# A six-tick distance between the issue of a load and the issue of its consumer, in a two-layer decoder trunk

## The chip, the cores and the metric

One NeuronCore of a Trainium2 chip runs the whole program. The metric is the device time of one execution in microseconds (us); lower is better. The kernel before took 1227.68 us, the median of three runs that lie between 1226.53 and 1230.73 us.

## What is computed

The reference is a decoder trunk of two layers on 256 tokens of width 1024, in float32. Each layer is a half-step feed-forward block, a token mixer and a second half-step feed-forward block; the mixer is forgetting attention ("fox") in layer 0 and a dilated windowed attention in layer 1. In front of each of these six blocks stands an RMS norm whose result is shifted and scaled, and behind it a gate, and shift, scale and gate come from a conditioning vector c:

```python
for i in range(DEPTH):
    mod = (silu(c) @ mod_w[i] + mod_b[i]).reshape(B, 3, 3, D)
    shift, scale, gate = mod[:, :, 0], mod[:, :, 1], mod[:, :, 2]
    h = modulate(rms_norm(x, norm_g[i, 0]), shift[:, 0], scale[:, 0])
    x = x + 0.5 * gate[:, 0] * swiglu(h, ffn_w_gate[i, 0], ffn_w_up[i, 0], ffn_w_down[i, 0])
    h = modulate(rms_norm(x, norm_g[i, 1]), shift[:, 1], scale[:, 1])
    y = fox_attention(h, ...) if i % 2 == 0 else dilated_attention(h, ...)
    x = x + gate[:, 1] * y
    h = modulate(rms_norm(x, norm_g[i, 2]), shift[:, 2], scale[:, 2])
    x = x + 0.5 * gate[:, 2] * swiglu(h, ffn_w_gate[i, 1], ffn_w_up[i, 1], ffn_w_down[i, 1])
```

All weights and the modulation matrix `mod_w` (2 x 1024 x 9216) are read from HBM once.

## The kernel before

**Products in parts.** Every float32 operand is split into a high part (rounded for the matmul's fast format) and a low part, the rest. A product of two matrices is three matmuls: high by high, high by low and low by high (`mm_blocks`, `mm_wide`, `mm3`, lines 382 to 404). ACT makes the high part of a weight (L207), VectorE (DVE) the low part (L216).

**Weight units.** `Weights` (line 175) holds a plan of all weight tiles in the order of their use, each a unit of up to 128 x 1024 elements. `load` (L189) issues the DMA of the next unit on SP into one of four buffers `raw`; `split_hi` and `split_lo` make `wh` and `wl`, of which there are seven pairs. Loading is tied to splitting: `split_lo` frees a `raw` buffer and calls `load` for the unit four ahead. `need` hands a unit to its products and splits it on the spot if that has not been done.

**Ticks.** The program is written out by Python in the order in which it stands on each engine. `tick` counts a step of the main work (a group of some six to twelve matmuls), lets `advance` issue at most one low and one high split, and then runs the events that `at(delay, ...)` has set for this tick. A tick is no time; it only says where in the program something is issued. PE and SP run strictly in the order of issue. DVE, ACT and GpSimd are arranged by a scheduler, from the same order of issue.

**Modulation steps.** `Mods` (line 257) computes the sixteen vectors of length 1024 that are not made in the opening. A vector takes eight steps. A step (L297) multiplies a 128 x 1024 tile of `mod_w`, in one of two buffers `mraw`, by a column of c and adds it to `acc`; `run` then issues, through `load` (L284), the load after next. When the eighth step is done, `finish` splits `acc` (for a vector of the fox stage: high part on ACT, L319, low part on DVE, L339) and four ticks later `spread` sums it over the partitions with matmuls against ones (L347 and L349, for two halves, four in all). The vectors are consumed by the norm and the gate at the end of a block. A `Pump` (line 363) is called once a unit and issues a step when the count falls behind its share:

```python
def go(self, want):
    if self.done < want and now[0] >= quiet[1]:
        ...
        vectors.run()

def flush(self):
    while self.done < self.n or vectors.open:
        self.go(self.n)
        tick()
```

**The end of a block.** `out_phase` runs the output products of all units but the last four, calls `pump.flush()`, and then runs the last four units' products half by half, with the gate, the sum and the next norm between them (`Boundary`). What `flush` issues on PE, the spread matmuls of the last vector among it, stands ahead of those last products.

**Fox.** The stage lasts from about 222 to 350 us. Its 24 modulation steps, the vectors (0,1,2), (0,2,0) and (0,2,1), are shared over 32 units. The attention of each group of four heads is issued by events: logits (L1140, L1141), the masked sum with its maximum on DVE (L960), the exponent on ACT (L962), transposes (L972), the values (L986), the reciprocal of the sums on DVE (L990), its spread by transposes (L1000), and the normalized output (L1003) with its low part (L1007).

Of the kernel before, what the change touches and what calls it, by code (L numbers as in the profile page):

```python
# [47 lines left out]
WBUFS = 7  # L48
# [12 lines left out]
NORM_FOX = 5  # L61
NORM_DIL = 10
RAWS = 4
AHEAD = 5
RI_DELAY = 1
QUIET0 = 5
# [26 lines left out]
def trunk_kernel(ctx, tc, x_in, c_in, positions, mod_w, mod_b, norm_g, w_gate, w_up, w_down,  # L93
# [25 lines left out]
    now = [0]  # L119
# [17 lines left out]
    def spread_out(delay, steps):  # L137

        def run():
            try:  # L140
                next(steps)
                at(2, run)
            except StopIteration:
                pass
        at(delay, run)

    def dram(t, off, ap):
        return bass.AP(tensor=t.tensor, offset=t.offset + off, ap=ap)
# [24 lines left out]
    quiet = [0, 0]  # L173

    class Weights:


        def __init__(self):
            self.plan, self.raws, self.parts, self.stamps = [], [], [], []
            self.loaded = self.hi = self.lo = self.used = self.live = 0  # L180
            self.started = False
            self.extra, self.spare = set(), None

        def load(self):
            if self.loaded < len(self.plan):
                shape, loads = self.plan[self.loaded]
                raw = rawp.tile([P] + shape, F32, tag="raw", bufs=RAWS, name="raw")
                for view, src in loads(raw):
                    nc.sync.dma_start(view, src)  # L189
                self.raws.append(raw)  # L190
                self.loaded += 1

        def start(self):
            self.started = True
            for _ in range(RAWS):
                self.load()
# [23 lines left out]
        def advance(self):  # L220
            if self.started and now[0] >= quiet[0]:
                if self.lo < self.hi and self.stamps[self.lo] < now[0]:
                    self.split_lo()
                spare = sum(i in self.extra for i in range(self.used, self.hi + 1))
                if self.hi < min(self.used + AHEAD + spare, self.loaded) and (
                        self.live < WBUFS or self.hi in self.extra):
                    self.split_hi()

        def need(self):
# [7 lines left out]
        def release(self):  # L237
            def run():
                self.live -= 1
            at(0, run)  # L240
# [4 lines left out]
    def behind(key, on=True):  # L245
        return tc.issue_after(ahead[key]) if on and key in ahead else ExitStack()
# [10 lines left out]
    class Mods:  # L257


        def __init__(self, order):  # L260
            self.steps = [(v, k) for v in order for k in range(KT)]
            self.loaded, self.done, self.open = 0, 0, 0
            self.raws = deque()

        def start(self):
            z = main.tile([P, D], F32, name="bias")
# [12 lines left out]
        def load(self):  # L279
            if self.loaded < len(self.steps):  # L280
                (l, s, j), k = self.steps[self.loaded]
                col = (s * 3 + j) * D
                raw = rawp.tile([P, D], F32, tag="mraw", bufs=2, name="mraw")
                nc.sync.dma_start(raw, mod_w[l, k * P:(k + 1) * P, col:col + D])  # L284
                self.raws.append(raw)
                self.loaded += 1

        def run(self):
            v, k = self.steps[self.done]
            l, s, j = v  # L290
            if k == 0:
                assert not self.open
                self.open += 1
                self.acc = main.tile([P, D], F32, tag="acc", bufs=1, name="acc")
            acc, raw = self.acc, self.raws.popleft()
            with behind("dve"):
                dve.scalar_tensor_tensor(acc, raw, ccol[:, k:k + 1], self.bias_tile if k == 0 else acc,  # L297
                                         op0=OP.mult, op1=OP.add)
            self.done += 1
            self.load()  # L300
            if k == 0:
                self.bias(self.done - 1 + KT)
            elif k == 2:
                dst = main.tile([P, D], F32, tag=f"mod{j}", name=f"mod{j}")
                if j == 1:
                    nc.sync.dma_start(dst, dram(norm_g, (l * 3 + s) * D, [[0, P], [1, D]]))
                mods[v] = dst
            elif k == KT - 1:
                self.finish(v, acc)
# [52 lines left out]
    class Pump:  # L362
# [7 lines left out]
            self.go(min(self.n, -(-self.n * self.seen // self.units)))  # L370

        def go(self, want):
            if self.done < want and now[0] >= quiet[1]:
                if vectors.open and vectors.steps[vectors.done][1] == 0:
                    return
                vectors.run()
                self.done += 1
# [6 lines left out]
    vectors = Mods(MODS_A + MODS_FOX + MODS_B + MODS_B2 + MODS_DIL + MODS_C)  # L384
# [322 lines left out]
    def open_trunk(wg, wu, pool):  # L707
# [54 lines left out]
        def load_weights(q):  # L762
            k0, n = groups[q]
            for k in range(k0, k0 + n):
                rows = slice(k * P, (k + 1) * P)
                raw = rawp.tile([P, 2, 512], F32, tag="raw", bufs=RAWS, name="raw")
                nc.sync.dma_start(raw[:, 0], wg[rows, 0:512])
                nc.sync.dma_start(raw[:, 1], wu[rows, 0:512])
                ws[0, k] = raw
                if k % 2 == 0:  # L770
                    raw = rawp.tile([P, 2, 512], F32, tag="raw", bufs=RAWS, name="raw")
                    nc.sync.dma_start(raw, wg[k * P:(k + 2) * P, 512:1024].rearrange("(k p) n -> p k n", p=P))
# [682 lines left out]
```

## Time and profile before

| what | value |
|---|---|
| median of three runs | 1227.68 us |
| the profiled execution | 1226.56 us |
| its span, first to last instruction | 1224.8 us |
| PE (TensorE matmul) busy | 1202.1 us, 98% |
| DVE (VectorE) busy | 952.3 us, 78% |
| ACT (ScalarE) busy | 665.0 us, 54% |
| read from HBM | 277.71 MB, 228 GB/s over the span |
| modulation loads: count, size, issue to landing | 128, 512 KB, 5.0 us |

PE counts matmuls as busy from their start to their modelled end, and neighbours overlap, so small gaps don't show in the share. The time of a wait is put down to the engine, or the DMA, whose signal came last. The profile's own execution is 1.1 us under the median.

### The profile page before, as it was taken

The numbers are of one execution on the slowest core, as the hardware profiler recorded it, in microseconds if no ns is written. First come the engines' busy times: TensorE is split into PE (matmuls) and PEld (weight loads), VectorE is DVE, ScalarE is ACT, GpSimd is POOL, SyncE is SP. The second block draws the span as 40 slices with busy tenths as digits, with TensorE's granted clock in tenths as the row PEclk, the third lists the DMA queues.
The fourth block names the chain that finished last, engine by engine and source line by source line (L and its number), as shares of the span: only waits on it lengthen the run. The fifth ranks groups of instructions, "written<-read, shape, count | busy, mean of one in ns | idle before, by whom it ended". The sixth has DMA issues, their size and how long they took to land.

```text
span 1224.8 us, 20467 instructions
## 1 busy us (share of the span) xinstructions
PE 1202.1 (98%) x7810; PEld 1071.1 (87%) x7810; DVE 952.3 (78%) x1362; ACT 665.0 (54%) x1038; POOL 99.0 (8%) x130
## 2 busy tenths in 40 slices
PE   6999999999999999999999999999999999999998
PEld 5999988878779999889999887888888787888887
DVE  7878777998788788569987659978786778877753
ACT  4446444576654555444554436577575655655540
POOL 1000000223100000001000004121131100000000
PEclk9999999999999999999999999999999999999999
DMA  9879986695839988638889656655645652877561
GB/s 332 274 260 341 307 306 196 190 309 192 283 98 345 324 275 311 212 111 288 307 270 331 205 172 215 214 190 165 225 146 188 207 172 86 273 215 221 172 214 41
DMA packets 162306, 281.16 MB, mean 230 GB/s; under 512 B 13424, under 2 KB 99984, under 8 KB 162208
## 3 DMA queue, kind: packets, MB, share of 16 engines
q1 hardware_dynamic: 162208, 279.85, 69.1%
q8 instruction: 61, 1.00, 0.3%
q14 instruction: 37, 0.30, 0.1%
HBM read 277.71 MB, written 2.10 MB: 228 GB/s over the span
## 4 chain that ended last, share of the span: by engine, by line
PE 78%; DVE 7%; DMA 5%; issue 4%; ACT 3%; POOL 2%; SPq 1%; POOLq 0%; DVEq 0%; ACTq 0%
PE bank L402 12%; PE bank L403 12%; PE bank L404 12%; PE block_bank L390 10%; PE block_bank L392 10%; PE block_bank L391 10%; PE block_bank L398 6%; PE block_bank L399 3%; DMA mraw<-in_mod_w_dram 3%; DVE wl L216 2%; POOL hrs L896 1%; ACT wh L207 1%; DVE lo L960 1%; DVE acc L297 1%; PE obank L986 1%
## 5 line engine op out<-in xcount | busy, mean ns | idle before, releaser
L216 DVE TENSOR_TENSOR wl<-raw,wh 128x1024 fp32r<-128x1024 f32 (+1 forms) x360 | 434.5, 1215 | 142.0 <-ACT wh L207 138.2
L207 ACT CAST wh<-raw 128x1024 fp32r<-128x1024 f32 (+1 forms) x360 | 374.0, 1045 | 263.2 <-PE bank L404 103.3
L390 PE MATMUL block_bank<-hT,wh 128*128 128x256 f32 x992 | 281.8, 284 | 2.0 <-ACT hT L819 2.0
L392 PE MATMUL block_bank<-hT,wl 128*128 128x256 f32 x992 | 281.7, 284 | 0.0
L391 PE MATMUL block_bank<-hT,wh 128*128 128x256 f32 x992 | 280.8, 283 | 0.0
L402 PE MATMUL bank<-wh,hT 128*128 128x512 f32 (+2 forms) x496 | 191.4, 386 | 1.1 <-DVE nm L960 0.7
L390 PEld LDWEIGHTS block_bank<-hT,wh 128*128 128x128 f32 x992 | 188.4, 190 | 2.4 <-ACT hT L819 2.1
L391 PEld LDWEIGHTS block_bank<-hT,wh 128*128 128x128 f32 x992 | 188.2, 190 | 0.5 <-DVE hT L822 0.2
L392 PEld LDWEIGHTS block_bank<-hT,wl 128*128 128x128 f32 x992 | 187.8, 189 | 0.0
L404 PE MATMUL bank<-wh,hT 128*128 128x512 f32 (+2 forms) x496 | 181.6, 366 | 0.0
L403 PE MATMUL bank<-wl,hT 128*128 128x512 f32 (+2 forms) x496 | 181.0, 365 | 0.0
L297 DVE SCALAR_TENSOR_TENSOR acc<-mraw,ccols,acc 128x1024 f32<-128x1024 f32 x112 | 143.3, 1280 | 31.5 <-DMA mraw<-in_mod_w_dram 31.3
L403 PE MATMUL bank<-wl,aTh 128*128 128x512 f32 (+1 forms) x420 | 146.4, 349 | 0.0
L402 PE MATMUL bank<-wh,aTh 128*128 128x512 f32 (+1 forms) x420 | 146.1, 348 | 0.0
L404 PE MATMUL bank<-wh,aTl 128*128 128x512 f32 (+1 forms) x420 | 145.7, 347 | 0.0
L398 PE MATMUL block_bank<-hT,wh 128*128 128x512 f32 x320 | 112.6, 394 | 0.0
L404 PEld LDWEIGHTS bank<-wh,hT 128*128 128x128 f32 x496 | 93.3, 188 | 16.5 <-DVE hT L479 0.5
L402 PEld LDWEIGHTS bank<-wh,hT 128*128 128x128 f32 x496 | 93.6, 189 | 15.8 <-issue 2.1
L403 PEld LDWEIGHTS bank<-wl,hT 128*128 128x128 f32 x496 | 93.7, 189 | 12.7
L399 PE MATMUL block_bank<-hT,wl 128*128 128x256 f32 x320 | 90.5, 283 | 0.0
L402 PEld LDWEIGHTS bank<-wh,aTh 128*128 128x128 f32 x420 | 79.5, 189 | 10.9
L404 PEld LDWEIGHTS bank<-wh,aTl 128*128 128x128 f32 x420 | 79.3, 189 | 10.5
(236 smaller groups left out, 1551.7 us busy)
## 6 DMA issues: line engine op xcount, KB each, us to landing
mraw<-in_mod_w_dram SPq DMA_DIRECT2D x128, 512.0 KB, 5.0
raw<-in_ffn_w_down_dram SPq DMA_DIRECT2D x88, 512.0 KB, 4.1
raw<-in_ffn_w_gate_dram SPq DMA_DIRECT2D x76, 512.0 KB, 4.6
raw<-in_ffn_w_up_dram SPq DMA_DIRECT2D x76, 512.0 KB, 4.2
raw<-in_dil_w_in_dram SPq DMA_DIRECT2D x128, 256.0 KB, 3.9
raw<-in_fox_w_in_dram SPq DMA_DIRECT2D x36, 256.0 KB, 4.3
oraw<-in_mod_w_dram SPq DMA_DIRECT2D x32, 256.0 KB, 6.3
raw<-in_ffn_w_gate_dram SPq DMA_DIRECT2D x24, 256.0 KB, 6.1
```

The costliest lines, as they stand in the source:

```text
L207: act.copy(wh, self.raws[self.hi])
L216: dve.tensor_sub(wl, self.raws[self.lo], wh.bitcast(F32))
L297: dve.scalar_tensor_tensor(acc, raw, ccol[:, k:k + 1], self.bias_tile if k == 0 else acc, op0=OP.mult, op1=OP.add)
L390: pe.matmul(out_i, wh[:, blk], hTh[:, :, k, :], start=first and i % 2 == 0, stop=False)
L391: pe.matmul(out_i, wh[:, blk], hTl[:, :, k, :], start=False, stop=False)
L392: pe.matmul(out_i, wl[:, blk], hTh[:, :, k, :], start=False, stop=last and i % 2 == 1)
L398: pe.matmul(o[i], wh[:, blk], hT[:, :, :, k, :], start=first, stop=False)
L399: pe.matmul(o[i][:, 0], wl[:, blk], hTh[:, :, k, :], start=False, stop=last)
L402: pe.matmul(o, ah, wh, start=first, stop=False)
L403: pe.matmul(o, ah, wl, start=False, stop=False)
L404: pe.matmul(o, al, wh, start=False, stop=last)
L896: nc.gpsimd.tensor_tensor(rs, ms, mhalf, op=OP.pow)
```

## The change

A constant `LANDED = 6` is added, and `Weights` and `Mods` note the tick at which each load is issued. `advance` issues the high split of a unit only if its load was issued six ticks ago or more; `need` still splits at once. The pump runs a modulation step only if the oldest load that no step has used was issued six ticks ago or more. `flush` keeps calling the pump, one tick at a time, until all steps of the stage are done. Nothing else is changed: the loads, the buffers, the splits and the steps are the same instructions, and only their places move.

```diff
--- before.py
+++ after.py
@@ -61,6 +61,7 @@
 NORM_FOX = 5
 NORM_DIL = 10
 RAWS = 4
+LANDED = 6
 AHEAD = 5
 RI_DELAY = 1
 QUIET0 = 5
@@ -176,7 +177,7 @@
 
 
         def __init__(self):
-            self.plan, self.raws, self.parts, self.stamps = [], [], [], []
+            self.plan, self.raws, self.parts, self.stamps, self.issued = [], [], [], [], []
             self.loaded = self.hi = self.lo = self.used = self.live = 0
             self.started = False
             self.extra, self.spare = set(), None
@@ -188,6 +189,7 @@
                 for view, src in loads(raw):
                     nc.sync.dma_start(view, src)
                 self.raws.append(raw)
+                self.issued.append(now[0])
                 self.loaded += 1
 
         def start(self):
@@ -223,7 +225,8 @@
                     self.split_lo()
                 spare = sum(i in self.extra for i in range(self.used, self.hi + 1))
                 if self.hi < min(self.used + AHEAD + spare, self.loaded) and (
-                        self.live < WBUFS or self.hi in self.extra):
+                        self.live < WBUFS or self.hi in self.extra) and (
+                        now[0] - self.issued[self.hi] >= LANDED):
                     self.split_hi()
 
         def need(self):
@@ -260,7 +263,10 @@
         def __init__(self, order):
             self.steps = [(v, k) for v in order for k in range(KT)]
             self.loaded, self.done, self.open = 0, 0, 0
-            self.raws = deque()
+            self.raws, self.issued = deque(), deque()
+
+        def landed(self):
+            return now[0] - self.issued[0] >= LANDED
 
         def start(self):
             z = main.tile([P, D], F32, name="bias")
@@ -283,6 +289,7 @@
                 raw = rawp.tile([P, D], F32, tag="mraw", bufs=2, name="mraw")
                 nc.sync.dma_start(raw, mod_w[l, k * P:(k + 1) * P, col:col + D])
                 self.raws.append(raw)
+                self.issued.append(now[0])
                 self.loaded += 1
 
         def run(self):
@@ -293,6 +300,7 @@
                 self.open += 1
                 self.acc = main.tile([P, D], F32, tag="acc", bufs=1, name="acc")
             acc, raw = self.acc, self.raws.popleft()
+            self.issued.popleft()
             with behind("dve"):
                 dve.scalar_tensor_tensor(acc, raw, ccol[:, k:k + 1], self.bias_tile if k == 0 else acc,
                                          op0=OP.mult, op1=OP.add)
@@ -370,7 +378,7 @@
             self.go(min(self.n, -(-self.n * self.seen // self.units)))
 
         def go(self, want):
-            if self.done < want and now[0] >= quiet[1]:
+            if self.done < want and now[0] >= quiet[1] and vectors.landed():
                 if vectors.open and vectors.steps[vectors.done][1] == 0:
                     return
                 vectors.run()
```

Line numbers of the change are higher than those before by 1 from line 64 on, by 2 from line 191, by 3 from line 227, by 6 from line 264, by 7 from line 286 and by 8 from line 296 on: L297 is L305 there, L339 is L347, L347 and L349 are L355 and L357, L1003 is L1011.

First piece: DVE at the end of the fox stage, from the last masked sum of the attention (`lo`) to the spread vector (`mod`). `acc` is the accumulator of a modulation step, `mraw` its loaded tile, `ri` the reciprocal, `on` and `oTl` the normalized heads. Before:

```order
L297 SCALAR_TENSOR_TENSOR acc<-mraw,ccols,acc 128x1024
L960 ISA lo,nm<-bank,table_972 128x256
L960 ISA nm 128x1
L339 TENSOR_TENSOR wl<-acc,wh 128x1024
L990 RECIPROCAL ri<-sums 128x8
L216 TENSOR_TENSOR wl<-raw,wh 128x1024
L351 SCALAR_TENSOR_TENSOR mod_3709<-bank,mod_3709 128x512
L1003 TENSOR_TENSOR on<-obank,on 128x512
```

With the change:

```order
L968 ISA lo,nm<-bank,table_953 128x256
L968 ISA nm 128x1
L218 TENSOR_TENSOR wl<-raw,wh 128x1024
L998 RECIPROCAL ri<-sums 128x8
L305 SCALAR_TENSOR_TENSOR acc<-mraw,ccols,acc 128x1024
L1011 TENSOR_TENSOR on<-obank,on 128x512
L305 SCALAR_TENSOR_TENSOR acc<-mraw,ccols,acc 128x1024
L1015 TENSOR_TENSOR oTl_2474<-on,oTh_2472 128x256
L1015 TENSOR_TENSOR oTl_2475<-on,oTh_2473 128x256
L305 SCALAR_TENSOR_TENSOR acc<-mraw,ccols,acc 128x1024 x4
L347 TENSOR_TENSOR wl<-acc,wh 128x1024
L218 TENSOR_TENSOR wl<-raw,wh 128x1024
```

Before, the last step and its low part (L339) stand ahead of the reciprocal; with the change six steps stand behind it, and the low part behind them.

Second piece: PE at the same place, from the transposes of the last head to the first product of the last four output units. Before:

```order
L972 MATMUL bank_3903<-ident,lo 128x128 x2
L986 MATMUL obank<-pt,v_3698 64x128 x4
L986 MATMUL obank<-pt,v_3699 64x128 x2
L1000 MATMUL rbank<-ident,wide 128x128 x4
L347 MATMUL bank<-wh,ones 128x512
L349 MATMUL bank<-wl,ones 128x512
L347 MATMUL bank<-wh,ones 128x512
L349 MATMUL bank<-wl,ones 128x512
L402 MATMUL bank<-wh,oTh_2472 128x512
```

With the change:

```order
L980 MATMUL bank_3870<-ident,lo 128x128 x2
L355 MATMUL bank<-wh,ones 128x512
L357 MATMUL bank<-wl,ones 128x512
L355 MATMUL bank<-wh,ones 128x512
L357 MATMUL bank<-wl,ones 128x512
L994 MATMUL obank<-pt,v_3672 64x128 x4
L994 MATMUL obank<-pt,v_3673 64x128 x2
L1008 MATMUL rbank<-ident,wide 128x128 x4
L355 MATMUL bank<-wh,ones 128x512
L357 MATMUL bank<-wl,ones 128x512
L355 MATMUL bank<-wh,ones 128x512
L357 MATMUL bank<-wl,ones 128x512
```

The spread of the vector (0,2,0) has moved down to here; the spread of the last vector, (0,2,1), and the products behind it keep their places. The only other move on PE is the spread of (0,1,2), some 70 matmuls later in the same stage.

Third piece: SP at the same place, where it issues the loads of modulation tiles among those of the next block's weights. Before:

```order
L284 DMA mraw<-in_mod_w_dram 128x1024
L189 DMA raw<-in_ffn_w_gate_dram 128x2x512
L284 DMA mraw<-in_mod_w_dram 128x1024 x2
L189 DMA raw<-in_ffn_w_gate_dram 128x2x512 x2
L189 DMA raw<-in_ffn_w_up_dram 128x2x512 x4
```

With the change:

```order
L290 DMA mraw<-in_mod_w_dram 128x1024
L283 DMA bias<-in_mod_b_dram 1x1024
L190 DMA raw<-in_ffn_w_gate_dram 128x2x512
L290 DMA mraw<-in_mod_w_dram 128x1024 x2
L314 DMA mod_3919<-in_norm_g_dram 128x1024
L290 DMA mraw<-in_mod_w_dram 128x1024 x5
L190 DMA raw<-in_ffn_w_gate_dram 128x2x512 x2
```

Seven loads of modulation tiles now stand between two loads of weights, where two stood.

## Rows read from the trace of the kernel before

**Rows 1.** The page, parts 1 and 4: busy time, and the chain that ended last.
```profile
PE 1202.1 (98%) x7810; PEld 1071.1 (87%) x7810; DVE 952.3 (78%) x1362; ACT 665.0 (54%) x1038; POOL 99.0 (8%) x130
...
PE 78%; DVE 7%; DMA 5%; issue 4%; ACT 3%; POOL 2%; SPq 1%; POOLq 0%; DVEq 0%; ACTq 0%
```
**Rows 2.** Windows, first feed-forward block and fox: stretch, length, each engine's busy us.
```profile
core 0: us, PE busy (x) PEld busy (x) DVE busy (x) ACT busy (x) POOL busy (x), PEclk, DMA share, GB/s
...
60.00:222.00 162.00, 161.98 (x1153) 152.23 (x1152) 128.89 (x135) 81.38 (x101) 3.55 (x7) 1.00 0.78 269
222.00:290.00 68.00, 65.83 (x386) 54.83 (x386) 61.95 (x102) 46.06 (x96) 16.50 (x12) 1.00 0.87 282
290.00:350.00 60.00, 57.89 (x379) 47.00 (x380) 45.89 (x88) 37.85 (x99) 10.34 (x17) 1.00 0.59 198
```
**Rows 3.** Waits of PE, 222 to 350 us: us in total, times, longest.
```profile
PE bank L921 <- DVE qn L900: 1.2, 1, 1.2
PE obank L986 <- ACT pt L974: 0.8, 1, 0.8
PE bank L402 <- DVE nm L960: 0.7, 1, 0.7
PE bank L1140 <- DVE ncum L1133: 0.6, 1, 0.6
PE bank L972 <- DVE nm L960: 0.5, 1, 0.5
PE bank L349 <- DVE wl L339: 0.3, 1, 0.3
PE bank L1140 <- DVE nm L960: 0.2, 1, 0.2
```
**Rows 4.** Waits of DVE for modulation loads: the whole run, then 222 to 350 us.
```profile
DVE acc L297 <- DMA mraw<-in_mod_w_dram: 31.3, 21, 3.5
...
DVE acc L297 <- DMA mraw<-in_mod_w_dram: 6.5, 3, 3.4
```
**Rows 5.** Timeline of DVE at the end of fox: start us, us, instruction [idle before].
```profile
308.50 1.28 DVE L297 SCALAR_TENSOR_TENSOR acc<-mraw,ccols,acc 128x1024 f32<-128x1024 f32 x1 [3.37 <-DMA mraw<-in_mod_w_dram]
...
328.60 1.28 DVE L297 SCALAR_TENSOR_TENSOR acc<-mraw,ccols,acc 128x1024 f32<-128x1024 f32 x1 [1.08 <-DMA mraw<-in_mod_w_dram]
...
335.62 1.23 DVE L339 TENSOR_TENSOR wl<-acc,wh 128x1024 fp32r<-128x1024 f32 x1 [0.77 <-ACT wh L319]
336.76 0.20 DVE L990 RECIPROCAL ri<-sums 128x8 f32<-128x8 f32 x1
...
341.23 0.68 DVE L1003 TENSOR_TENSOR on<-obank,on 128x512 f32<-128x512 f32 x1
...
342.43 0.75 DVE L1007 TENSOR_TENSOR oTl<-on,oTh 128x256 fp32r<-128x256 f32 x2
```
**Rows 6.** The chain that ended last, 318 to 346 us: start us, us, what.
```profile
339.53 0.59 PE rbank L1000 x4
340.12 0.23 PE bank L347
...
340.82 0.24 PE bank L349
341.06 0.23 PE bank L402
```
**Rows 7.** All uses of the tile mraw: durations min/median/max, and its loads.
```profile
L297 DVE SCALAR_TENSOR_TENSOR acc<-mraw,ccols,acc x112: 1267/1279/1308, 73.2 to 1122.7; 128x1024 f32<-128x1024 f32 x112
...
DMA to landing us min/median/max: 3.7/5.0/7.9
```
**Rows 8.** Timeline of ACT at the end of fox.
```profile
334.54 1.05 ACT L319 CAST wh<-acc 128x1024 fp32r<-128x1024 f32 x1 [0.95 <-DVE acc L297]
```
**Rows 9.** Windows in the opening, columns as in group 2.
```profile
19.90:24.80 4.90, 4.84 (x21) 4.64 (x22) 4.41 (x8) 1.31 (x3) 0.00 (x0) 1.00 1.07 373
24.90:29.80 4.90, 4.90 (x44) 4.90 (x44) 4.83 (x11) 1.64 (x2) 0.00 (x0) 1.00 1.09 355
```

## Prediction

> **What bounds the kernel now.** I read the busy shares first: TensorE is busy for 98% of the span, and the chain that ended last is 78% PE, 7% DVE and 5% DMA [rows 1]. So time can be won only where PE waits, and lost wherever something new makes it wait. The table by stage says where that is: from 60 to 222 us, the first feed-forward block, PE is busy for 161.98 of 162.00 us; in the forgetting attention (fox) it misses 2.17 us of 68 and 2.11 of 60 [rows 2]. The waits of PE in the fox stage show seven waits, 4.3 us together, none behind a DMA directly [rows 3]. VectorE does wait for the modulation loads: 31.3 us over the run, but only 6.5 of that in fox, where PE can feel it [rows 4]. Two of those waits reach PE: the steps that start at 308.50 and 328.60 stood 3.37 and 1.08 us idle before them [rows 5], and the logits behind them on DVE hold PE for 0.7 and 0.5 us [rows 3].
>
> **The change part by part.** It removes no instruction and adds none; a load keeps its size and each step its operation. It moves the point at which a step enters the program, and that is read from the built order.
>
> *Splits.* In the feed-forward and dilated stages they move by a tick or so, and the PE order there is unchanged. At the first block the splits of units 0 to 4 are issued 5 to 8 ticks later, yet on DVE the splits of the first six units stay ahead of all modulation steps. What hides them is that PE runs these blocks without a gap [rows 2] and splits stay at least one tick ahead of their use. I cost them at nothing; if that cover were gone, each late unit would cost at most one split of 1.2 us. In the dilated stage the modulation steps keep their ticks: they come six ticks or more apart already. No gain there.
>
> *Modulation steps in fox.* The pump spreads 24 steps over 32 units of two ticks, one each 2.7 ticks. There are two load buffers, and a step's run issues the load after next; with the gate a pair of steps takes six ticks or more, three per step, and the pump never catches up. When the output phase flushes the pump, 22 of 24 steps were issued before; with the change 16 are. All eight steps of the last vector (call them 40 to 47) then stand together. On PE nothing has given way: the four matmuls that spread this vector still stand behind the transposes of the last heads and ahead of the 48 products of the last four output units, as the second piece of order shows. PE takes them in order.
>
> So the chain is: load, step, load, step, through two buffers. I follow it on the clock of the trace. Steps 40 and 41 fall between the last logits and start the loads of 42 and 43, which land before they are wanted. Step 42 stands behind the reciprocal, which ends at 336.96 [rows 5]; a step takes 1.28 us [rows 7], so it ends at 338.3 and releases load 44. Step 43 stands behind the product of L1003, which ends at 341.91 [rows 5]: it ends at 343.2 and releases load 45. The two low parts (L1007) take 0.75 us [rows 5], and step 44 follows to 345.2, releasing load 46. From there each load counts from issue to landing: 3.7 us at least, 5.0 median, 7.9 at most [rows 7]. I take 4.4, between the least and the median, because SP has nothing to issue in this stretch except these loads. Load 45 lands at 347.6, step 45 ends at 348.9; load 46 lands at 349.6, step 46 ends at 350.9; load 47, released at 348.9, lands at 353.3 and step 47 ends at 354.6. Then come ACT's cast, 1.05 us [rows 8], the low part on DVE, 1.23 us [rows 5], and after the first spread matmul three more of 0.23 us [rows 6]. The last products start at 357.6 instead of 341.06 [rows 6]: **+16.5 us**. With 3.7 us landings (two on the path) it is +15.1, with 5.0 it is +17.7, with 7.9 it is +23.5.
>
> *The clock.* In that wait PE has nothing between the end of the last transposes at 340.12 [rows 6] and 355.65, some 15.5 us. The trace before has no such idle stretch once PE runs. Its nearest row is the start: after a beginning with little work PE issues 21 matmuls in the 4.9 us from 19.9, and 44 in the 4.9 us from 24.9 [rows 9], about half the pace, as the 1.2 GHz level gives against 2.4; the clock column reads 1.00 in both rows, so I go by the pace. That is worth 4.9 x (1 - 21/44) = 2.6 us. The ends are 0, if the clock stays, and 2.6; I take 2.6, since 15.5 us idle is nearer to the idle start than to a stage without gaps. By the Trainium skill, "TensorE: Matmul & The Clock Gate", section "What's actually happening", the slow level is what an idle PE returns to and work releases it; by it the 2.6 stay in the sum, but no row here shows the clock falling a second time inside the run.
>
> *What is won.* The two PE waits behind late modulation loads in fox, 0.7 + 0.5 = **-1.2 us** [rows 3]; at most all 4.3.
>
> The sum is 16.5 + 2.6 - 1.2 = **+17.9 us**. The profiled execution took 1226.56 us (its span is 1224.8), so it would become 1244.5. The median of the runs before, 1227.68, lies 1.1 above it; on the median I forecast **1245.5 us**.
>
> **The rivals.** *Hidden, and faster.* DVE no longer stands in front of unlanded data, and its 31.3 us of waiting [rows 4] goes. The Trainium skill, "DMA: Bandwidth & Descriptors", section "Rules for kernel authors", tells authors to issue a DMA early, compute, and wait for it late, and the gate does wait later. By that rule alone the time would fall; but here the run of a step is also what issues a later load, so the gate delays issues as well as waits. In rows: PE could get back 1.2 to 4.3 us in fox [rows 3], for 1223.4 to 1226.5, say 1223.5. It decides in the flush: step 47 would have to end before PE ends the last transposes at 340.12 [rows 6]. Against it, two steps and two whole landings still follow step 43, which cannot end before 343.2. Chance 0.03.
>
> *No difference.* The late steps and the saved waits cancel, within 0.3% (about 3.7 us, what a measurement of this kernel can tell from no change). It would need a stall of under 5 us in the flush, where one landing with its step is 5 already and there are two. Chance 0.04.
>
> *The clock stays.* All as forecast, without the 2.6: 1242.9 us. For it speaks that the clock is shown only at full level after the start, against it that PE was never idle so long. Chance 0.15.
>
> *Contended loads.* The loads in the flush take the 7.9 us of the longest row [rows 7], because weight loads for the next block are still being moved: +7.0, so 1252.5 us. Against it, the four weight buffers fill early and their next loads wait for splits. Chance 0.08.
>
> The forecast itself keeps 0.70.
>
> **How the numbers follow.** The low end takes landings of 3.7 (-1.4), no fall of the clock (-2.6) and all 4.3 us of PE waits won (-3.1): +10.8, or 1238.5; rounded down, 1238. The high end takes landings of 5.0 (+1.2), nothing won (+1.2) and one longest landing on the path in place of a median one (+2.9): +23.2, or 1251. The forecast and the case with the clock at full level lie inside, 0.85 together. Slower by over 0.3%: 0.70 + 0.15 + 0.08 = 0.93. Within 0.3%: 0.04. Faster: 0.03.
>
> **What the profile of the change would show.** On PE, one idle stretch of about 15 us at the end of fox, in front of the spread matmuls, released by the cast of the accumulator or by its low part, and the same order as before around it. On DVE, four steps in a row there with two waits of 2 to 4 us for the modulation load, and hardly any wait for it earlier in fox. After the stretch, products at half pace for some us if the clock falls. From 60 to 222 us and in the dilated stage, PE as busy as before. I am wrong if that stretch is under 5 us, if PE waits for split weights in a feed-forward block, or if the time is gained back in the dilated stage.

## Result, and the profile after

The change takes 1242.72 us, the median of four runs (1241.27 to 1243.61), against 1227.99 us for the kernel before in the same session: a ratio of 1.0116, 95% interval 1.0096 to 1.0137. It is slower by 14.7 us; forecast were 1245.5 us, in a range of 1238 to 1251, and slower. The profiled execution of the change took 1243.61 us, its span is 1241.9.

The page of the change, parts 1, 2 (one row) and 4, answers to [rows 1]:

```profile
PE 1203.3 (97%) x7810; PEld 1070.7 (86%) x7810; DVE 952.5 (77%) x1362; ACT 665.3 (54%) x1038; POOL 96.1 (8%) x130
...
PEclk8999999999979999999999999999999999999999
...
PE 76%; DVE 8%; DMA 6%; issue 4%; ACT 3%; POOL 2%; SPq 1%; POOLq 0%; DVEq 0%; ACTq 0%
```

The work is the same to the instruction, and PE is busy 1.2 us longer in a span 17.1 us longer: it waits. One slice in forty has a granted clock of 7 tenths; before, no slice inside the run fell. The windows place both (columns as in [rows 2]):

```profile
core 0: us, PE busy (x) PEld busy (x) DVE busy (x) ACT busy (x) POOL busy (x), PEclk, DMA share, GB/s
60.00:222.00 162.00, 161.99 (x1152) 152.15 (x1151) 128.41 (x134) 81.44 (x100) 3.56 (x7) 1.00 0.79 268
...
341.00:352.00 11.00, 0.57 (x1) 0.29 (x1) 5.71 (x6) 1.66 (x2) 0.00 (x0) 0.50 0.72 198
352.00:358.00 6.00, 5.53 (x14) 4.15 (x14) 4.25 (x5) 1.37 (x2) 0.00 (x0) 0.50 0.61 174
358.00:365.00 7.00, 7.00 (x32) 5.71 (x31) 4.62 (x8) 1.45 (x4) 0.55 (x1) 1.00 0.18 67
```

The first feed-forward block is as full as before. From 341 to 352 us PE runs a single matmul, and the granted clock is at its lower level, 1.2 GHz; in the next six us it runs 14 matmuls at 1.2 GHz, and only then is the clock back at 2.4. The waits of PE from 222 to 366 us answer to [rows 3] (us in total, times, longest):

```profile
PE bank L355 <- ACT wh L327: 13.6, 1, 13.6
PE bank L980 <- ACT lo L970: 1.0, 2, 0.7
```

The two waits of 0.7 and 0.5 us behind the attention's maximum [rows 3] are gone, 1.0 us behind its exponent is new, and one of 13.6 us is there: the spread of the last vector waits for the high part of the accumulator. DVE's waits for modulation loads, in the whole run and then from 222 to 366 us:

```profile
DVE acc L305 <- DMA mraw<-in_mod_w_dram: 34.8, 25, 3.1
...
DVE acc L305 <- DMA mraw<-in_mod_w_dram: 8.0, 6, 1.8
```

The gate was to keep steps away from loads that have not landed, yet the total is 34.8 us where it was 31.3 [rows 4]; a second profile of the change (experiment 6) has 33.3. The timeline of DVE at the end of fox shows where the waits are now (start, us, instruction, idle before it):

```profile
339.13 1.27 DVE L305 SCALAR_TENSOR_TENSOR acc<-mraw,ccols,acc 128x1024 f32<-128x1024 f32 x1
340.32 0.75 DVE L1015 TENSOR_TENSOR oTl<-on,oTh 128x256 fp32r<-128x256 f32 x2
340.99 1.28 DVE L305 SCALAR_TENSOR_TENSOR acc<-mraw,ccols,acc 128x1024 f32<-128x1024 f32 x1
344.04 1.28 DVE L305 SCALAR_TENSOR_TENSOR acc<-mraw,ccols,acc 128x1024 f32<-128x1024 f32 x1 [1.77 <-DMA mraw<-in_mod_w_dram]
346.63 1.28 DVE L305 SCALAR_TENSOR_TENSOR acc<-mraw,ccols,acc 128x1024 f32<-128x1024 f32 x1 [1.31 <-DMA mraw<-in_mod_w_dram]
349.02 1.28 DVE L305 SCALAR_TENSOR_TENSOR acc<-mraw,ccols,acc 128x1024 f32<-128x1024 f32 x1 [1.10 <-DMA mraw<-in_mod_w_dram]
351.41 1.23 DVE L347 TENSOR_TENSOR wl<-acc,wh 128x1024 fp32r<-128x1024 f32 x1 [1.11 <-ACT wh L327]
```

Steps 43 to 47 stand here, all but the first behind the low parts of the last heads (L1015), the last three each behind a load. The chain that ended last goes through every second of them (start, us, what):

```profile
337.22 0.60 PE rbank L1008 x4
...
340.43 3.51 DMA mraw<-in_mod_w_dram
...
344.04 1.30 DVE acc L305
...
345.35 3.58 DMA mraw<-in_mod_w_dram
...
349.02 1.29 DVE acc L305
...
350.34 1.05 ACT wh L327
...
351.41 1.24 DVE wl L347
...
352.69 0.79 PE bank L357
353.49 0.43 PE bank L355
353.92 0.43 PE bank L357
354.34 0.43 PE bank L410
```

Step 43 ends and load 45 is issued; it lands, step 45 runs, load 47 is issued; it lands, step 47 runs; then cast, low part, spread, and the first product at 354.34, where it stood at 341.06 [rows 6].

Where the time lies can be read from the start of the same matmul in both profiles. One at the end of the first feed-forward block is 0.4 us earlier (222.25 and 221.88 us), one at the end of fox's output 14.8 later (350.37 and 365.14), one at the end of the third feed-forward block still 14.7 later (731.38 and 746.09), the last of all 17.0 later (1220.85 and 1237.89). Fox costs 15.1 us, the feed-forward blocks nothing; 2.3 us more come in the dilated stage of this execution.

### The profile page after: what moved, and what is told of

The parts are those of the page before. It is cut to its first block, busy times and chain, and to the rows that moved or that the text cites. A ratio compares the mean times of both kernels' runs of the same rounds, so it can differ in the third digit from the quotient of the medians.

```text
span 1241.9 us, 20469 instructions
## 1 busy us (share of the span) xinstructions
PE 1203.3 (97%) x7810; PEld 1070.7 (86%) x7810; DVE 952.5 (77%) x1362; ACT 665.3 (54%) x1038; POOL 96.1 (8%) x130
## 4 chain that ended last, share of the span: by engine, by line
PE 76%; DVE 8%; DMA 6%; issue 4%; ACT 3%; POOL 2%; SPq 1%; POOLq 0%; DVEq 0%; ACTq 0%
PE bank L410 11%; PE bank L411 11%; PE bank L412 11%; PE block_bank L400 9%; PE block_bank L398 9%; PE block_bank L399 9%; PE block_bank L406 6%; DMA mraw<-in_mod_w_dram 3%; PE block_bank L407 3%; DVE wl L218 3%; POOL hrs L904 1%; DMA raw<-in_dil_w_in_dram 1%; PE obank L994 1%; PE bank L980 1%; DVE acc L305 1%
## 5 line engine op out<-in xcount | busy, mean ns | idle before, releaser
L305 DVE SCALAR_TENSOR_TENSOR acc<-mraw,ccols,acc 128x1024 f32<-128x1024 f32 x112 | 143.4, 1281 | 35.1 <-DMA mraw<-in_mod_w_dram 34.8
```

## Experiments

The theory is the one of the prediction: with two buffers, and a step that issues the load after next, the gate limits the pump to two steps in six ticks, eight steps are left for the flush, and there they run at the pace of load and step ahead of PE's last products. The rivals: the gate on splits is to blame; the empty ticks of the longer flush are; the idle PE's clock is most of it; the loads themselves are slow there. Each ratio is against runs of the kernel before on the same chip in the same session.

**1. Only the splits gated.**

```diff
-            if self.done < want and now[0] >= quiet[1] and vectors.landed():
+            if self.done < want and now[0] >= quiet[1]:
```

> Only the splits of weight units keep the gate; modulation steps run as before. The backlog theory (the lost time is the eight modulation steps left for the flush of the fox stage) expects the time of before, within 0.3% (1224 to 1232 us), 22 of 24 steps issued at the flush, and no PE wait over 2 us at the end of fox. The rival that late splits cost time expects a part of the 14.7 us here, 3 us or more, with PE waiting behind the low part of a split. For the 2.3 us by which the dilated stage became longer: if they come from the splits' places, they are here too.

Measured: 1229.18 us, ratio 1.0014 (1.0004 to 1.0024), +1.7 us by the ratio; 22 of 24 steps are issued when fox is flushed, and the longest PE wait in fox is 1.4 us. The splits are not the cause of the loss; by the median they are not quite free either.

**2. Only the steps gated.**

```diff
-                        self.live < WBUFS or self.hi in self.extra) and (
-                        now[0] - self.issued[self.hi] >= LANDED):
+                        self.live < WBUFS or self.hi in self.extra):
```

> Only the modulation steps keep the gate; splits are issued as before. The backlog theory expects the time of the change, 1240 to 1245 us, with the one PE wait of 12 to 15 us ahead of the last spread matmuls of fox and the clock down behind it. The rival of late splits expects 3 us or more less than the change. If the 2.3 us in the dilated stage are here and not in the run with gated splits alone, they come with the steps.

Measured: 1241.63 us, 1.0124 (1.0108 to 1.0139), and the wait of PE is there to the tenth:

```profile
PE bank L354 <- ACT wh L326: 13.6, 1, 13.6
```

The steps carry the whole loss.

**3. Steps gated, but the flush calls them without the gate**, so it takes 13 ticks and not 25.

```diff
-        def go(self, want):
-            if self.done < want and now[0] >= quiet[1] and vectors.landed():
+        def go(self, want, late=False):
+            if self.done < want and now[0] >= quiet[1] and (late or vectors.landed()):
...
-                self.go(self.n)
+                self.go(self.n, True)
```

> The change, but the flush issues its steps without asking for the six ticks: it takes 13 ticks in place of 25. The eight steps are still left for it. The backlog theory (real loads through two buffers set the wait, ticks set none) expects the time of the change, 1240 to 1245 us, and a PE wait of 12 to 15 us. The rival that the flush's own ticks cost the time expects half of it back, about 1235 us.

Measured: 1242.8 us, 1.0129 (1.0114 to 1.0144), one PE wait of 13.9 us. Empty ticks cost nothing; the steps that are left over do.

**4. The distance: four ticks for both, four and eight for the steps alone.**

```diff
-LANDED = 6
+LANDED = 4
```

> The change with a distance of four ticks in place of six, for splits and steps: a pair of steps in four ticks, two a step, which is faster than the 2.7 that the pump asks for, so 22 of 24 steps are issued at the flush, as before. The backlog theory expects the time of before or up to 0.3% less (1222 to 1231 us) and no PE wait over 2 us at the end of fox. The rival that any gate costs, by moving steps on DVE, expects 5 us or more of the loss to stay.

Measured: 1226.62 us, 0.9998 (0.9988 to 1.0007), 22 of 24 steps issued at the flush, no PE wait in fox over 1.4 us.

> Only the steps gated, at four ticks: 22 of 24 issued at the flush, splits as before. The backlog theory expects no difference from before that is over 0.3%. If data that has landed when its step comes up is worth something, it shows here and nowhere else: DVE's 31.3 us of waits for modulation loads should fall, and PE's two waits behind them, 1.2 us, should go: 1225 to 1227 us. If waits of DVE that PE does not feel are worth nothing, the time is that of before.

Measured: 1227.73 us, 1.0005 (0.9996 to 1.0014). The gain that a gate should bring without a backlog does not come. Nor did it remove waits; DVE's over the run, which were 31.3 in 21 [rows 4], with the steps alone gated (36.2 with both gates at four ticks):

```profile
DVE acc L304 <- DMA mraw<-in_mod_w_dram: 33.3, 23, 3.8
```

With `LANDED = 8` and the steps alone:

> Only the steps gated, at eight ticks in place of six: 14 of 24 steps are issued at the flush of fox, ten are left, and at the flush of the first feed-forward block two are left where none was. The backlog theory prices a further pair of steps through two buffers at 4.9 us (3.5 landing, 1.28 step and the hand-overs, as in the profile of the change), and the two steps in the first block at 1 to 5 us of cast, low part and spread: 1246 to 1254 us. A rival by which the wait in fox is a fixed price of the flush expects 1242 us.

Measured: 1248.57 us, 1.0169 (1.0151 to 1.0187). 14 of 24 steps are issued at fox's flush, and the first feed-forward block has a backlog of its own, 22 of 24; the end of that block comes 4.6 us later than before. Both show as waits of PE:

```profile
PE bank L354 <- ACT wh L326: 15.7, 1, 15.7
...
PE bank L354 <- DVE wh L340: 3.1, 1, 3.1
```

With the steps alone gated, four, six and eight ticks leave two, eight and ten steps to the flush of fox. In one profile each, the stage is 2.5, 15.5 (experiment 2) and 18.5 us longer than before. The 2.5 are not at the flush but ahead of it (see the last section), and the median of that version is the one of before; stages of single profiles differ by some 2 us (experiment 6). The fifth pair cost 3.0 us, not the 4.9 expected, and the chain of the eight-tick run shows that no third landing was added (start, us, what):

```profile
345.23 1.27 DVE acc L304
...
347.18 1.21 DVE acc L304
...
348.40 4.76 DMA mraw<-in_mod_w_dram
...
353.25 1.29 DVE acc L304
...
354.56 3.50 DMA mraw<-in_mod_w_dram
...
358.16 1.29 DVE acc L304
```

Two landings are on the path, as in the change. What is longer is the stretch ahead of the first, where steps 42 and 43 now both stand behind the product of the last heads (`on`), by 1.9 us, and the landings themselves, 4.85 and 3.60 to the start of the step, by 1.2.

**5. The clock: PE filled with unread matmuls while the steps run.** Their results are used by nothing. First 54, three in a tick:

```diff
         def flush(self):
+            start, db = now[0], None
...
+                if now[0] > start + 7:
+                    db = db or bank()
+                    for _ in range(3):
+                        pe.matmul(db, ones, hTh[:, 0, 0:4, :].rearrange("p k n -> p (k n)"), start=True, stop=True)
```

> The change, with 54 matmuls of 512 columns that nobody reads, issued on PE in the flush of fox between the last transposes and the last spread: 54 x 0.232 = 12.5 us of the 13.6 us that PE waits there. If the granted clock fell because PE was idle, it stays up, the 12 or so matmuls behind the wait run at 0.232 in place of 0.43 us, and the time falls by 2 to 3 us, to about 1240 us. If the clock falls for another reason, the time is that of the change, 1242 to 1243 us. Added work, nothing left out.

Measured: 1245.59 us, 1.0146 (1.0131 to 1.0162). Inconclusive: the fill was too short. It ended at 349.97 us, the high part was ready only at 352.93, the clock fell in between, and three of the unread matmuls stood behind the spread, where they cost time. The second version puts 64 ahead of the spread:

```diff
+                if start + 8 < now[0] and vectors.open:
+                    db = db or bank()
+                    for _ in range(4):
+                        pe.matmul(db, ones, hTh[:, 0, 0:4, :].rearrange("p k n -> p (k n)"), start=True, stop=True)
```

> As the run with 54 unread matmuls, but 64 of them, all ahead of the last spread: 64 x 0.232 = 14.8 us, which covers the wait of 13 to 15 us to its end. If idleness of PE lowers the clock, there is now no stretch at half pace behind the wait, the first products run at 0.232 us, and the time is 2 to 3 us below that of the change (about 1240 us). If the clock falls all the same, or the fill delays the spread by more than it saves, it is 1242 us or more. Added work, nothing left out.

Measured: 1240.06 us, 1.0107 (1.0093 to 1.0121). Windows, and the timeline of PE:

```profile
341.00:352.00 11.00, 11.00 (x49) 9.03 (x49) 5.98 (x7) 0.29 (x1) 0.00 (x0) 1.00 0.69 203
352.00:358.00 6.00, 5.24 (x22) 3.86 (x21) 4.89 (x6) 3.05 (x3) 0.00 (x0) 1.00 0.52 145
```

```profile
338.89 14.92 PE L395 MATMUL bank<-hT,ones 128*128 128x512 f32 x64
...
355.71 0.40 PE L415 MATMUL bank<-wh,oTh 128*128 128x512 f32 x1
355.95 0.39 PE L416 MATMUL bank<-wl,oTh 128*128 128x512 f32 x1
```

The clock stays at 2.4 GHz, and products follow each other after 0.23 us, not 0.43. The first of them even starts 1.5 us later than in the change, yet fox is 0.9 us shorter than in the first profile of the change, and 2.6 shorter than in the second. The median is 2.7 us lower; by the ratios, each to its own session, it is 1.1 us against the first measurement of the change and 2.8 against its repeat (experiment 6), with overlapping intervals. So the size rests on the trace; that it is a small part of the loss, and that the wait for the steps is the large one, both measurements say.

**6. The change again**, without an edit.

> The change itself once more, for a second profile. In the first, the dilated stage was 2.3 us longer than before, though its modulation steps keep their ticks. If that is the changed order of DVE and ACT there, it comes back within 0.5 us; if it is a difference between executions, the second profile shows another number. The wait at the end of fox should be 13 to 14.5 us again.

Measured: 1243.17 us, 1.0130 (1.0112 to 1.0149), a PE wait of 14.6 us; fox costs 16.8 us in this profile and the dilated stage 0.6; with the steps alone gated (experiment 2) that stage is 1.2 us shorter than before. So the 2.3 us of the first profile in the dilated stage differ between executions and are no effect of the change that these runs can tell.

**7. A third load buffer in the fox stage.** With both gates left at six ticks, every third load of the stage goes to a buffer of its own:

```diff
+                if self.third and self.loaded % 3 == 2:
+                    if self.loaded >= 48:
+                        return
+                    raw = self.third.tile([P, D], F32, tag="mraw3", bufs=1, name="mraw3")
+                else:
+                    raw = rawp.tile([P, D], F32, tag="mraw", bufs=2, name="mraw")
...
         pump = Pump(MODS_FOX, PUMP_FOX)
+        vectors.third = pool
+        vectors.load()
```

> The change with six ticks kept everywhere, and a third buffer for modulation tiles in the fox stage alone: three steps in six ticks, two a step, so 22 of 24 are issued at the flush. The backlog theory (rate = buffers over distance) expects the time of before within 0.3% (1224 to 1231 us) and no PE wait over 2 us at the end of fox, though every step still waits its six ticks. The rival that the six ticks themselves cost the time expects 1240 us or more.

Measured: 1230.8 us, 1.0031 (1.0021 to 1.0041). 22 of 24 steps are issued at the flush, and no PE wait in fox exceeds 1.6 us. The gate is as long as in the change, and with three steps in six ticks 11 of the 15 us are gone. Then the same buffer with the steps alone gated:

> The third load buffer in the fox stage with the six-tick gate on the modulation steps only; the splits of weight units are issued freely as in the kernel before. With both gates this buffer left 3.8 us. Theory (the backlog of the steps is gone with the third buffer, and what is left belongs to the gate on splits, 1.7 us by itself): about 2 us above the kernel before, 1228 to 1229.5, no wait of TensorE over 3 us at the end of fox. Rival (what is left belongs to the gated steps, with or without the splits): 3 us or more above, 1230 to 1231.5. If it comes out at the kernel before, the splits and the buffer explain all of the remainder.

Measured: 1227.19 us, 0.9998 (0.9989 to 1.0007). A gate of six ticks on the steps costs nothing once the buffers keep the pace, and what the first run of experiment 7 had left belongs to the gate on splits. In the profiles 2.8 us of it are in fox, in several places. One window of each, first with both gates, then with the steps alone:

```profile
246.00:254.00 8.00, 6.22 (x30) 4.61 (x29) 7.97 (x13) 4.42 (x6) 0.00 (x0) 1.00 1.04 366
```

```profile
246.00:254.00 8.00, 7.33 (x34) 5.49 (x32) 7.93 (x14) 4.23 (x7) 0.00 (x0) 1.00 1.03 355
```

Four matmuls fewer, 1.1 us less of PE: at 253.87 us the first logits have waited 1.6 us for `ncum`, in the other run 0.3. The rest are short waits later in fox, mostly behind the attention's exponent (2.8 and 0.9 us). Which late splits cause them was not traced.

**8. The third buffer alone, in the kernel before.**

> The kernel before, without a gate, with the third buffer in fox. DVE's 6.5 us of waits for modulation loads in fox should mostly go, and with them the two PE waits behind them, 1.2 us: 1225 to 1227 us. If it is faster than before beyond its interval, it is the version to keep; if not, DVE's waits in fox were worth nothing to PE.

Measured: 1227.55 us, 1.0006 (0.9997 to 1.0015), DVE's waits in fox 5.7 us after 6.5 [rows 4]. The waits that should mostly have gone are nearly all there, so the run does not show what their absence would be worth. No version beats the kernel before; a third buffer for the whole program was not tried.

## Why the prediction was right

**What bounds the kernel.** Right: the total of DVE's waiting, 31.3 us before [rows 4], does not tell the time. It is 41.2 us in experiment 1, at 1229.18 us, and 33.3 in the repeat of the change, at 1243.17. The time follows the one long wait that PE has, and the part of DVE's waits that stands in front of it. What the 31.3 us would be worth if they were gone is not shown: no version removed them.

**The chain in the flush**, forecast +16.5 us. From the end of the last transposes to the first product there were 0.94 us before [rows 6]; now there are 354.34 - 337.82 = 16.52. Of the 15.6 more, 0.7 belong to the clock: the three spread matmuls behind the low part took 1.65 us, and 0.97 with the gap filled (experiment 5). The chain is worth 14.9. The links are those that were forecast: the two landings on the path, steps 45 and 47, cast, low part. The term that was mis-sized is the landing: I took 4.4 us, and from the issue of the load to the start of its step the two took 3.61 (340.43 to 344.04) and 3.67 (345.35 to 349.02): the least of the run before [rows 7], for which the prediction had +15.1. That is not a fixed size: in the repeat (experiment 6) the two took 3.64 and 4.57, and the chain 15.8 us. The reason given, that SP issues nothing else there, pointed the right way: between 338 and 352 us SP issues five loads of modulation tiles and nothing else. A load of 7.9 us, the rival, did not occur.

**The clock**, forecast +2.6. The spreads' 0.7 and, until 357.98 us, some 8.5 products at 0.2 us more each, 1.7, make 2.4. The forecast's way to 2.6 was not sound: of the 44 matmuls in its second window [rows 9], 16 have a single column, so 21 against 44 is not the pace of one kind.

```profile
26.65 1.84 PE L806 MATMUL bank<-ones,cacc 128*128 128x1 f32 x16
```

The products of 256 columns in the two windows follow each other after 0.21 and 0.12 us, which makes 2.0 us for 21 of them; that 2.6 came so near is in part luck. Going by the pace and not by the clock column was right: in the profile of the change the column reads 0.50 in that stretch of the opening.

```profile
17.00:23.00 6.00, 3.19 (x13) 3.00 (x14) 5.36 (x13) 1.66 (x3) 0.00 (x0) 0.50 1.09 355
```

That the clock falls inside the run was forecast without a row that showed it. Now rows do: 0.50 while PE is idle and behind that, 1.00 with the same gap filled. By the Trainium skill, "TensorE: Matmul & The Clock Gate", section "What's actually happening", an idle PE returns to the slow level; the trace agrees. The rival in which the clock stays would have given 1242.9 us and lies nearer to the median than the forecast, but it has the wrong cause: the fall is in the trace, and the shorter landings hide it in the total.

**What is won**, forecast -1.2. The two waits named are gone, and the transposes end 2.3 us earlier, of which 0.4 came with the opening: -1.9. The sum is then 14.9 + 2.4 - 1.9 = 15.4 us, against 15.1 seen in the starts. The -1.9 is one profile's; in the repeat it is -1.0.

**The splits, costed at nothing.** Slightly wrong, and so is the reason: that PE runs the feed-forward blocks without a gap is true, and the cost is elsewhere, in fox. By themselves they cost 1.7 us (experiment 1), with the third buffer about 4, the difference between the ratios of the two runs of experiment 7. Beside the stall nothing of it shows: the ratio is 1.0124 without that gate (experiment 2) and 1.0116 with it, inside both intervals.

**The signs.** The stretch on PE came as forecast, 13.6 us and a second wait of 0.5. On DVE I named four steps with two waits of 2 to 4 us and hardly any wait earlier in fox. There are three waits of 1.1 to 1.8 us, 4.2 together, since two loads are always on their way, one half a period behind the other; and 3.8 us of waiting remain earlier. Ticks are not time, and a gate in ticks does not remove waits for a load.

**The rule that spoke for the change.** The Trainium skill, "DMA: Bandwidth & Descriptors", section "Rules for kernel authors", tells authors to issue a DMA early and wait for it late. The trace shows where that ends: here the late wait also issues a load, and waiting later made the loads late. With a third buffer, which lets three loads fall into the same distance, the loss is gone, and there is still no gain.

## What to carry to other kernels

A distance of so many steps between issue and use, with n buffers that are refilled by the use, is a limit on the rate: n uses in that distance. Compare it with the rate that the consumer needs; what it cannot keep up with is left for the place where the work must be done, and if that place stands in order ahead of the bounding engine's next work, that engine waits for the last of it. Count the landings that then stand one behind the other: here eight steps put two on the path, and two steps more added none. Before an idle time of an engine off the path is removed, look for who waits for that engine; here the total of 31 us moved up and down by some us without the time following it.

## What the runs showed of the hardware that was not expected

Useless work did not cost time, and probably won some: with 64 unread matmuls in the gap of the change, 14.92 us of PE time, the median was 1240.06 us and not 1242.72. The clock was at 2.4 GHz when the products came, which experiment 5 shows in the trace; the intervals of the two ratios overlap.

And the clock fell inside fox without any long wait. In the four-tick version, windows around it:

```profile
322.00:325.60 3.60, 2.03 (x12) 1.19 (x11) 2.68 (x6) 1.43 (x5) 0.00 (x0) 0.99 1.06 383
325.60:329.00 3.40, 3.40 (x15) 2.09 (x14) 2.55 (x4) 1.64 (x5) 0.00 (x0) 0.51 0.86 304
329.00:332.00 3.00, 3.00 (x22) 2.59 (x20) 1.88 (x5) 1.71 (x4) 0.00 (x0) 1.00 0.55 139
```

PE was busy for 2.03 of 3.60 us, with no wait over 1.4 us, and then ran 3.4 us at 1.2 GHz: products of 512 columns followed each other after 0.43 us, 0.23 in the window behind. With the steps alone gated at four ticks the same fall stands at the same place (0.50 from 325.5 to 328.9 us). It does not follow from such a stretch alone. Experiment 1, with the same wait of 1.4 us at 324.78, kept its clock:

```profile
322.00:325.60 3.60, 1.98 (x12) 1.05 (x11) 2.97 (x6) 1.05 (x4) 0.00 (x0) 1.00 1.06 378
325.60:329.00 3.40, 3.40 (x23) 2.60 (x24) 1.89 (x4) 1.90 (x6) 0.00 (x0) 1.00 0.96 336
```

What decides is open. Matmul by matmul, the four-tick version falls 3.6 us behind the kernel before between 308 and 327 us, 1.5 of them while the clock is low, and ends fox 2.6 us behind; its median, 0.9998 of before, does not show it.
